# Accumulating on copied PSUM banks, an accumulating DMA for one weight sum, and a reordered opening in a hybrid decoder block

## The chip, the cores and the metric

The kernel runs on one core of a Trainium2 chip. A core has a matrix engine (TensorE, PE in the profile, with its weight loads as PEld), a vector engine (VectorE, DVE), a scalar engine (ScalarE, ACT), GpSimd (POOL) and a queue engine that issues transfers (SyncE, SP). Transfers run on 16 DMA engines, whichever queue issues them. TensorE writes its products into PSUM, eight banks of 512 float32 columns on 128 partitions. The metric is the device time of one execution in microseconds (us), as a median of runs.

## The reference

One decoder layer on 256 tokens of width 2048, in float32: a half-step SwiGLU feed-forward part, a mixer, a second half-step SwiGLU feed-forward part, and a closing norm.

```python
def swiglu_ffn(x, w_gate, w_up, w_down):
    return (jax.nn.silu(x @ w_gate) * (x @ w_up)) @ w_down
...
        x = x + FFN_RESIDUAL_SCALE * swiglu_ffn(rms_norm(x, ffn1_norm[l]), ...)
        z = rms_norm(x, mix_norm[l]) @ w_in[l]
...
        x = x + y @ w_out[l]
        x = x + FFN_RESIDUAL_SCALE * swiglu_ffn(rms_norm(x, ffn2_norm[l]), ...)
    return rms_norm(x, final_norm)
```

Between `z` and `y` stand a gated linear recurrence and a short convolution. The feed-forward width is 5632, so each of the two parts multiplies by 2048x5632, 2048x5632 and 5632x2048 matrices. These products are most of the work.

## The kernel before

**Splits.** Every float32 operand is split into a high part, rounded to the matrix engine's float32r format, and the lower part that is left. A product is three matmuls: high by high, low by high, high by low. A weight tile of 512 rows by 512 columns is a *unit*: `load` (line 155) fetches it over SP's queue, 1 MB, into a slot of the pool `raws` (three slots) or, where it is marked `kept`, of a pool of two slots (tag `kept`). `parts_of` (169) makes the high part on ACT in two casts of 128x1024 and the lower part on DVE in one subtraction of 128x2048. There are two or three slots for split tiles. `multiply` (194) runs all products with the high weight part ahead of those with the lower: 8 and 4 matmuls of 512 columns for each target.

**Products.** `product` (286) multiplies both token halves (t = 0, 1) by a column block of 512, over units. `seven` (326) does a block of 1024 columns and 1024 rows with seven products of half the size in place of eight, in the manner of Strassen and Winograd, and adds the rest of the rows with ordinary units. Its accumulators are the PSUM banks a, c, e and d. The products are numbered 0, 4, 5, 6, 2, 3, 1 in their order. Product 0 takes the weight quarter w11 into a, product 4 the sum w12 - w11 into c; then the ordinary unit b2 goes into e and c (the *two-target block* of the prediction); then product 5 adds to a, and so on. DVE makes four sums of weight quarters (128x2048 each) in a block. ACT copies a and c to SBUF four times in between (`snap`, 342: s1, s5, u2, u3), and DVE adds these at the end:

```python
        dve.tensor_tensor(u3, u3, s5, op=ALU.add)
        dve.tensor_tensor(u3, e, u3, op=ALU.add)
        dve.tensor_tensor(u2, c, u2, op=ALU.add)
        dve.tensor_tensor(s1, d, s1, op=ALU.add)
```

w11 and w12 lie in the two `kept` slots, and the slot of either goes to the next block when its last use is through.

**A feed-forward part** (`ffn`, 384) begins with one ordinary gate product of 512 columns and one ordinary up product. Ten sevens (gate and up, five times, s = 0 to 4) do the other ten column blocks, and after s = 0, 2 and 4 `down` (460) multiplies what has come about so far by the down weights: `product` for column block 0, a seven for blocks 1 and 2, `product` for block 3. That makes 13 sevens a part, 26 in all. The down products are added to the residual `xres` by DVE (`update`, 463). `settle` turns hidden tiles by PE transposes (tiles `ph`) through PSUM.

**The opening of a part.** The first products run on the unnormalised input, and their results are scaled afterwards. The sevens need the normalised input, since they add tiles of it: `norm.rows` (243) spreads the row factors over the partitions with two small products (`pb_n`) and a copy (`bc_n`); then the tiles v (line 433, both `kept` slots) are formed, scaled, split into x, and `seven_of` (308) forms the sums of the seven products' other operands (`xs`). In the program all this stands between the gate product and the up product. In the first part the gate product is `opening` (542), whose instructions are held to program order on each engine (`Engine.pinned`).

**Order.** Elsewhere the framework's planner orders each engine's instructions: it walks through time by its own estimates and gives a free engine the ready instruction that stands first in the program. The engines then run these rows in order, with semaphores. All PSUM tiles come from one pool of eight banks (79). Line 42 in the profile is the helper through which every PE, DVE and ACT instruction passes, and L164 is the load.

## Time and profile before

| | us |
|---|---|
| median of three runs (1776.07 to 1777.52) | 1777.3 |
| the profiled execution | 1779.27 |
| its span, first to last instruction | 1777.3 |
| PE busy | 1744.6 (98%) |
| DVE busy | 1494.4 (84%) |
| ACT busy | 1046.8 (59%) |
| POOL busy | 6.9 |

The span is what the profiler saw of one execution, 2.0 below that execution's time. Busy time of PE is the time in which a matmul was under way. Matmuls are pipelined, so a single one of 512 columns lasts 0.39 us in the records while in a stream one ends every 0.23. In a row of the timeline stand the start, the length, engine and line, operation, output and inputs by the program's names, shape, and the number of instructions merged; in brackets the engine's idle time ahead of it and what ended it. `ps_g_a` is bank a of a gate seven, `hi_g_p` and `lo_g_p` the split parts of a unit for one of its seven products, `hi_g_x` those of an ordinary unit; u and d stand for up and down.

### The profile page before, as it was taken

The page shows a single profiled execution, that of the slowest core. Times are in us where ns is not written, and L with a number is a line of the kernel's source. Part 1 is how long each engine was busy: PE and PEld are TensorE (multiplying, and loading weights), DVE is VectorE, ACT ScalarE, POOL GpSimd, SP SyncE. Part 2 cuts the span into 40 slices and gives each one's busy share as a digit, 9 for nine tenths or more (in the row PEclk, how much of TensorE's full clock was granted, in tenths as well). Part 3 has the DMA queues.
Part 4 walks back from the last instruction along what each step waited for, and adds up shares of the span by engine and source line. Part 5 has one row for each costly group of instructions (what it writes and reads, how often), then busy time and mean ns, then how long its engine had stood idle before and what let it go on. Part 6 is the DMA issues. An engine that isn't in the chain of part 4 may idle for free. (4 is left out here: it accounts for less than half of the span.)

```text
span 1777.3 us, 20302 instructions
## 1 busy us (share of the span) xinstructions
PE 1744.6 (98%) x8031; PEld 1441.5 (81%) x8031; DVE 1494.4 (84%) x1221; ACT 1046.8 (59%) x1342; POOL 6.9 (0%) x32
## 2 busy tenths in 40 slices
PE   7999999999999999999999999999999999999998
PEld 5787888888888888888888887887888888888886
DVE  6898989989789888688987667989899887899895
ACT  6565556656465656575765554656566664556664
POOL 1000000000000000000000000000000000000000
PEclk9999999999999999999999999999999999999999
DMA  7366655574566574456565655574566637555743
GB/s 249 132 214 212 213 189 190 190 245 155 186 196 209 172 256 166 145 188 196 175 196 170 209 189 190 190 242 157 192 214 202 209 135 259 189 190 190 257 158 106
DMA packets 173905, 343.24 MB, mean 193 GB/s; under 512 B 5621, under 2 KB 8049, under 8 KB 173681
## 3 DMA queue, kind: packets, MB, share of 16 engines
q1 hardware_dynamic: 173344, 340.82, 57.2%
q8 instruction: 63, 1.03, 0.2%
q10 hardware_dynamic: 144, 1.05, 0.2%
q14 instruction: 34, 0.27, 0.0%
q0 software_dynamic: 320, 0.07, 0.0%
HBM read 339.82 MB, written 2.10 MB: 192 GB/s over the span
## 5 line engine op out<-in xcount | busy, mean ns | idle before, releaser
L42 PE MATMUL ps_in<-xT_nm,hi_in 128*128 128x512 f32 x640 | 224.1, 395 | 0.0
L42 ACT CAST hi_g_p<-raw_g 128x1024 fp32r<-128x1024 f32 x140 | 140.5, 1048 | 123.4 <-DVE raw_g L42 40.9
L42 DVE TENSOR_TENSOR lo_g_p<-raw_g,hi_g_p 128x2048 fp32r<-128x2048 f32 x70 | 159.7, 2287 | 36.0 <-ACT hi_g_p L42 35.5
L42 ACT CAST hi_u_p<-raw_u 128x1024 fp32r<-128x1024 f32 x140 | 141.5, 1049 | 66.3 <-PE ps_u_a L42 25.9
L42 PE MATMUL ps_in<-xT_nm,lo_in 128*128 128x256 f32 x640 | 178.6, 281 | 0.6 <-DVE lo_in L42 0.6
L42 DVE TENSOR_TENSOR lo_u_p<-raw_u,hi_u_p 128x2048 fp32r<-128x2048 f32 x70 | 159.2, 2286 | 22.2 <-ACT hi_u_p L42 22.1
L42 PE MATMUL ps_d<-hi_d,h 128*128 128x512 f32 x704 | 172.2, 396 | 2.8 <-DVE h L42 2.2
L42 PEld LDWEIGHTS ps_d<-hi_d,h 128*128 128x128 f32 x704 | 132.6, 189 | 33.3 <-DVE h L42 3.0
L42 PEld LDWEIGHTS ps_in<-xT_nm,hi_in 128*128 128x128 f32 x640 | 119.8, 187 | 27.1
L42 ACT CAST hi_d<-raw_d 128x1024 fp32r<-128x1024 f32 x88 | 88.0, 1048 | 81.9 <-PE ps_u_d L42 25.3
L42 DVE TENSOR_TENSOR lo_d<-raw_d,hi_d 128x2048 fp32r<-128x2048 f32 x44 | 100.7, 2289 | 31.7 <-ACT hi_d L42 31.7
L42 PEld LDWEIGHTS ps_in<-xT_nm,lo_in 128*128 128x128 f32 x640 | 120.6, 189 | 1.4 <-DVE lo_in L42 1.1
L42 DVE TENSOR_TENSOR lo_in<-raw_in,hi_in 128x2048 fp32r<-128x2048 f32 x40 | 91.4, 2285 | 32.7 <-ACT hi_in L42 32.5
L42 ACT CAST hi_in<-raw_in 128x1024 fp32r<-128x1024 f32 x80 | 81.5, 1049 | 62.1 <-PE ps_in L42 48.8
L42 ACT CAST hi_d_p<-raw_d 128x1024 fp32r<-128x1024 f32 x84 | 84.5, 1048 | 48.2 <-DVE raw_d L42 21.0
L42 DVE TENSOR_TENSOR lo_d_p<-raw_d,hi_d_p 128x2048 fp32r<-128x2048 f32 x42 | 95.5, 2287 | 18.9 <-ACT hi_d_p L42 18.8
L42 ACT CAST hi_g_x<-raw_g 128x1024 fp32r<-128x1024 f32 x80 | 80.8, 1049 | 41.2 <-PE ps_g_c L42 19.9
L42 ACT CAST hi_u_x<-raw_u 128x1024 fp32r<-128x1024 f32 x80 | 80.6, 1049 | 37.3 <-PE ps_u_c L42 25.8
L42 DVE TENSOR_TENSOR raw_u<-raw_u,raw_u 128x2048 f32<-128x2048 f32 x40 | 91.6, 2291 | 9.4 <-DMA raw_u<-in_ffn_w_up_dram 8.7
L42 DVE TENSOR_TENSOR raw_g<-raw_g,raw_g 128x2048 f32<-128x2048 f32 x40 | 91.5, 2287 | 6.4 <-DMA raw_g<-in_ffn_w_gate_dram 5.8
L42 DVE TENSOR_TENSOR lo_g_x<-raw_g,hi_g_x 128x2048 fp32r<-128x2048 f32 x40 | 91.4, 2286 | 3.8 <-ACT hi_g_x L42 3.7
L42 DVE TENSOR_TENSOR lo_u_x<-raw_u,hi_u_x 128x2048 fp32r<-128x2048 f32 x40 | 91.5, 2287 | 3.7 <-ACT hi_u_x L42 3.1
(349 smaller groups left out, 3612.5 us busy)
## 6 DMA issues: line engine op xcount, KB each, us to landing
raw_u<-in_ffn_w_up_dram SPq DMA_DIRECT2D x88, 1024.0 KB, 5.3
raw_d<-in_ffn_w_down_dram SPq DMA_DIRECT2D x88, 1024.0 KB, 5.1
raw_g<-in_ffn_w_gate_dram SPq DMA_DIRECT2D x87, 1024.0 KB, 5.3
raw_in<-in_w_in_dram SPq DMA_DIRECT2D x40, 1024.0 KB, 5.1
raw_o<-in_w_out_dram SPq DMA_DIRECT2D x16, 1024.0 KB, 5.1
xres<-in_x_dram SPq DMA_DIRECT2D x4, 512.0 KB, 8.3
fin<-in_final_norm_dram ACTq DMA_DIRECT2D x1, 1024.0 KB, 4.7
out_dram<-xres SPq DMA_DIRECT2D x4, 256.0 KB, 2.7
```

Of the source, the lines that this page charges most:

```text
L42: ins = getattr(self.engine, name)(*args, **kwargs)
```

## The change

1. **Copied banks.** In a seven, ACT copies bank a onto bank d after product 0 and bank c onto bank e after product 4, in place of two snapshots, and the later matmuls add onto the copies. Two of the four additions on DVE go. For this the matmuls of e and d no longer begin a bank, and PSUM is divided: for each feed-forward part six `full` banks for accumulators, each written once by a dummy product of zeros, and two `part` banks for transposes and small products (`small`); for the mixer one pool of eight. In `down`, ACT writes twice the residual into the banks of an ordinary product first, and half of the result back to the residual, in place of DVE's update; the last product of the kernel keeps the old form. A down seven adds its parts to the residual one by one.
2. **The accumulating DMA.** w12 is loaded ahead of w11, and a second DMA, issued on POOL's queue, reads w11 from memory and adds it to w12. Product 4 takes this sum directly. The other three sums of a block stay on DVE.
3. **Signs.** To make that sum possible some operands are negative: the ordinary units of the second column half and one operand of the seven are split with a factor of -1, and the results of the second half are used with -1.
4. **The opening.** `norm.rows`, the tiles v and x and `seven_of` move from between the gate and the up product into the up product, one step after each of its units (`normalise`). In `opening`, units 1 to 3 are split by halves: a cast and a subtraction of half the size, twice.

```diff
--- before.py
+++ after.py
-    psum = ctx.enter_context(tc.tile_pool(name="psum", bufs=8, space=bass.MemoryType.PSUM))
-
-    def bank(name):
-        return psum.tile([P, 512], F32, tag="ps", name=name)
+    pools = {}
+
+    @contextmanager
+    def banks(name, parts):
+        with ExitStack() as st:
+            for kind, n in (("full", 8 - parts), ("part", parts)):
+                if n:
+                    pools[kind] = st.enter_context(
+                        tc.tile_pool(name=f"{kind}_{name}", bufs=n, space=bass.MemoryType.PSUM)
+                    )
+            if parts:
+                for i in range(8 - parts):
+                    pe.matmul(bank(f"first_{name}_{i}"), zeros[:, :P], zeros, start=True, stop=True)
+            else:
+                pools["part"] = pools["full"]
+            yield
+
+    def bank(name, kind="full"):
+        return pools[kind].tile([P, 512], F32, tag="ps", name=name)
+
+    def small(name):
+        return bank(name, "part")
...
+    zeros = const.tile([P, 512], F32R, name="zeros")
+    dve.memset(f32(zeros), 0.0)
...
+    ffn1_banks = ExitStack()
+    ffn1_banks.enter_context(banks("ffn1", 2))
...
         for i, e in pieces:
             if split:
                 split(i)
-            act.copy(hi[:, i:e, :], raw[:, i:e, :])
+            if minus:
+                act.activation(hi[:, i:e, :], raw[:, i:e, :], AF.Copy, scale=-1.0)
+            else:
+                act.copy(hi[:, i:e, :], raw[:, i:e, :])
             if split:
                 dve.tensor_tensor(lo[:, i:e, :], raw[:, i:e, :], f32(hi[:, i:e, :]), op=ALU.subtract)
-        if not split:
+        if minus:
+            dve.scalar_tensor_tensor(lo, raw, -1.0, f32(hi), op0=ALU.mult, op1=ALU.subtract)
+        elif not split:
             dve.tensor_tensor(lo, raw, f32(hi), op=ALU.subtract)
         return [(hi[:, j, :], lo[:, j, :]) for j in range(UK)]
...
-                pt = bank(f"pt_{self.name}_{k}")[:, :S]
+                pt = small(f"pt_{self.name}_{k}")[:, :S]
...
-    def product(w, c, us, y, name, stagger=False, between=None):
+    def product(w, c, us, y, name, stagger=False, between=None, base=None):
+
         ps = [bank(f"ps_{name}_{t}") for t in range(NT)]
+        if base:
+            for t in range(NT):
+                act.activation(ps[t], base(t), AF.Copy, scale=2.0)
...
-            begin, end = i == 0, i == len(us) - 1
+            begin, end = i == 0 and not base, i == len(us) - 1
+                multiply([(ps[t], stationary(y(u), t), begin, end) for t in range(NT)], blk, base is not None)
...
-        dve.tensor_tensor(spare, a21, a22, op=ALU.add)
+        dve.tensor_tensor(spare, a22, a21, op=ALU.subtract)
         dve.tensor_tensor(a21, a11, a21, op=ALU.subtract)
-        dve.tensor_tensor(a11, spare, a11, op=ALU.subtract)
-        dve.tensor_tensor(a12, a12, a11, op=ALU.subtract)
+        dve.tensor_tensor(a11, spare, a11, op=ALU.add)
+        dve.tensor_tensor(a12, a11, a12, op=ALU.subtract)
         for (i, q), (hi, lo) in zip(((4, spare), (5, a11), (6, a21), (2, a12)), parts):
-            act.copy(hi, q)
-            dve.tensor_tensor(lo, q, f32(hi), op=ALU.subtract)
+            if i == 5:
+                act.activation(hi, q, AF.Copy, scale=-1.0)
+                dve.scalar_tensor_tensor(lo, q, -1.0, f32(hi), op0=ALU.mult, op1=ALU.subtract)
+            else:
+                act.copy(hi, q)
+                dve.tensor_tensor(lo, q, f32(hi), op=ALU.subtract)
...
-        w11, w12 = get(r0, 0, True), get(r0, 1, True)
+        w12, w11 = get(r0, 1, True), get(r0, 0, True)
+        nc.gpsimd.dma_start(w12, at(r0, 0).rearrange("(j p) c -> p j c", p=P), accum_op=ALU.add)
...
-            blk = parts_of(raw, f"{name}_x{i}{n}")
+            blk = parts_of(raw, f"{name}_x{i}{n}", minus=n == 1)
             multiply([(ps, stationary(xs[i][1], t), b, z) for ps, t, b, z in targets], blk, True)
         product_of(0, w11, a, True)
-        s1 = snap(a, "s1")
-        dve.tensor_tensor(w11, w12, w11, op=ALU.subtract)
-        product_of(4, w11, c, True)
-        s5 = snap(c, "s5")
-        usual(0, b2, 1, (e, 1, True, not two), (c, 0, False, False))
-        dve.tensor_tensor(w11, w22, w11, op=ALU.subtract)
-        product_of(5, w11, a)
+        act.copy(d, a)
+        product_of(4, w12, c, True)
+        act.copy(e, c)
+        usual(0, b2, 1, (e, 1, False, not two), (c, 0, False, False))
+        dve.tensor_tensor(w12, w22, w12, op=ALU.add)
+        product_of(5, w12, a)
         u2 = snap(a, "u2")
         if between:
             between()
         if two:
             usual(1, b3, 1, (e, 1, False, True), (c, 0, False, False))
-        dve.tensor_tensor(w12, w22, w12, op=ALU.subtract)
-        product_of(6, w12, a)
+        dve.tensor_tensor(w11, w12, w11, op=ALU.subtract)
+        product_of(6, w11, a)
         u3 = snap(a, "u3")
         product_of(2, w22, c)
-        usual(0, a2, 0, (d, 0, True, False), (a, 1, False, False))
-        dve.tensor_tensor(w11, w21, w11, op=ALU.subtract)
-        product_of(3, w11, a, end=not two)
+        usual(0, a2, 0, (d, 0, False, False), (a, 1, False, False))
+        dve.tensor_tensor(w12, w21, w12, op=ALU.add)
+        product_of(3, w12, a, end=not two)
         if two:
             usual(1, a3, 0, (a, 1, False, True), (d, 0, False, False))
         product_of(1, w21, d)
-        dve.tensor_tensor(u3, u3, s5, op=ALU.add)
-        dve.tensor_tensor(u3, e, u3, op=ALU.add)
-        dve.tensor_tensor(u2, c, u2, op=ALU.add)
-        dve.tensor_tensor(s1, d, s1, op=ALU.add)
-        return {(1, 1): u3, (0, 1): u2, (1, 0): a, (0, 0): s1}
+        return {(1, 1): (e, u3), (0, 1): (c, u2), (1, 0): (a, None), (0, 0): (d, None)}
...
-                pt = bank(f"ph{tag}_{u}_{t}")
+                pt = small(f"ph{tag}_{u}_{t}")
...
-            norm.rows()
+            xs, sf = [], {}
+
+            def normalise(u):
+                if u == 0:
+                    norm.rows()
+                bcs = norm.bc.unsqueeze(1).to_broadcast([P, UK, S])
...
-                    sf = seven_of(
+                    sf.update(seven_of(
...
+                    ))
+
+            pu = product(wu, 0, range(4), norm.xT.__getitem__, f"u{tag}_0", between=normalise)
             xs = list(enumerate(xs))[2:]
-            pu = product(wu, 0, range(4), norm.xT.__getitem__, f"u{tag}_0")
...
-                def update(c, t, ps):
-                    xr = xres[:, t, c * CW : (c + 1) * CW]
-                    Engine.pinned = last and tag == 2 and c == NC_D - 1
-                    dve.scalar_tensor_tensor(xr, ps, 0.5, xr, op0=ALU.mult, op1=ALU.add)
-                    if last:
-                        after(c, t)
+                def columns_of(c, t):
+                    return xres[:, t, c * CW : (c + 1) * CW]
 
                 for c in (0, 3):
                     end = last and tag == 2 and c == NC_D - 1
                     ps = product(
-                        wd, c, us, hidden.get, f"d{tag}_{us[0]}_{c}", end, (lambda i: settle()) if c == 0 else None
+                        wd, c, us, hidden.get, f"d{tag}_{us[0]}_{c}", end, (lambda i: settle()) if c == 0 else None,
+                        None if end else lambda t: columns_of(c, t),
                     )
                     for t in range(NT):
-                        update(c, t, ps[t])
+                        xr = columns_of(c, t)
+                        if end:
+                            Engine.pinned = True
+                            dve.scalar_tensor_tensor(xr, ps[t], 0.5, xr, op0=ALU.mult, op1=ALU.add)
+                        else:
+                            act.activation(xr, ps[t], AF.Copy, scale=0.5)
+                        if last:
+                            after(c, t)
...
-                                update(c1, t, q[t, c1 - 1])
+                                xr = columns_of(c1, t)
+                                for part in q[t, c1 - 1]:
+                                    if part is not None:
+                                        dve.scalar_tensor_tensor(xr, part, 1.5 - c1, xr, op0=ALU.mult, op1=ALU.add)
+                                if last:
+                                    after(c1, t)
...
                 g = seven(wg, (0, 1), c0, sf, xs, f"g{tag}_{s}", keep, settle)
-                for q in ((1, 1), (0, 1), (1, 0), (0, 0)):
-                    if q == (1, 0):
-                        z = keep(f"z{tag}_{s}")
-                        act.activation(z, g[q], AF.Silu)
-                        g[q] = z
+                for q in QUADS:
+                    ps, z = g[q]
+                    if z is None:
+                        z = keep(f"z{tag}_{s}_{q[0]}")
                     else:
-                        act.activation(g[q], g[q], AF.Silu)
+                        dve.tensor_tensor(z, ps, z, op=ALU.add)
+                        ps = z
+                    act.activation(z, ps, AF.Silu, scale=-1.0 if q[1] else 1.0)
+                    g[q] = z
                 h = seven(wu, (0, 1), c0, sf, xs, f"u{tag}_{s}", keep)
-                for t, n in ((1, 1), (0, 1), (1, 0), (0, 0)):
-                    dve.tensor_tensor(g[t, n], h[t, n], g[t, n], op=ALU.mult)
+                for t, n in QUADS:
+                    ps, z = h[t, n]
+                    if z is not None:
+                        dve.tensor_tensor(z, ps, z, op=ALU.add)
+                        ps = z
+                    if n:
+                        dve.scalar_tensor_tensor(g[t, n], ps, -1.0, g[t, n], op0=ALU.mult, op1=ALU.mult)
+                    else:
+                        dve.tensor_tensor(g[t, n], ps, g[t, n], op=ALU.mult)
                     waiting.append((1 + 2 * s + n, t, g[t, n], s % 2 == 0))
...
-                blk = unit(src, f"g1_0_{u}")
+                halves_of = ((0, 2), (2, 4))
+                blk = parts_of(load(src, f"g1_0_{u}"), f"g1_0_{u}", halves_of, lambda i: None)
...
-    with tc.tile_pool(name="mixer", bufs=1) as mp, tc.tile_pool(name="mixw", bufs=2) as mw:
+    ffn1_banks.close()
+    with tc.tile_pool(name="mixer", bufs=1) as mp, tc.tile_pool(name="mixw", bufs=2) as mw, banks("mixer", 0):
...
-    ffn(2, n2, last)
+    with banks("ffn2", 2):
+        ffn(2, n2, last)
...
```

31 lines of the change are left out of this document (14 added, 17 removed).

## The prediction

> **What bounds the kernel now.** I read the head of the page first, then a table of stretches, then TensorE's (PE's) waits, and only then the timeline around the waits that matter. The first fence is the head of the page, with the span and the busy time of each engine. The second is the table of stretches: start:end, length, and for each engine its busy time and number of instructions, then granted clock, share of the DMA engines and GB/s.
>
> ```profile
> span 1777.3 us, 20302 instructions
> PE 1744.6 (98%) x8031; PEld 1441.5 (81%) x8031; DVE 1494.4 (84%) x1221; ACT 1046.8 (59%) x1342; POOL 6.9 (0%) x32
> ```
>
> ```profile
> 0.00:80.00 80.00, 63.05 (x255) 49.75 (x256) 56.45 (x71) 46.45 (x73) 5.87 (x16) 0.94 0.58 198
> 80.00:1040.00 960.00, 957.53 (x4576) 799.29 (x4575) 811.68 (x719) 571.53 (x757) 1.05 (x16) 1.00 0.58 193
> 1040.00:1130.00 90.00, 87.21 (x387) 70.61 (x386) 71.66 (x65) 50.91 (x65) 0.00 (x0) 0.98 0.54 177
> 1130.00:1750.00 620.00, 618.33 (x2739) 506.97 (x2738) 543.42 (x345) 367.18 (x426) 0.00 (x0) 1.00 0.59 200
> 1750.00:1778.00 28.00, 18.51 (x81) 14.83 (x79) 11.24 (x25) 10.77 (x23) 0.00 (x0) 0.92 0.21 76
> ```
>
> PE is busy for all but 32.7 us. In the long stretches 80 to 1040 and 1130 to 1750 it is idle for 2.5 and 1.7 us, and there VectorE (DVE) at 85 to 88% holds nobody up. So work taken from DVE inside the blocks is worth at most some 4 us. Idle time that a change could win lies in the first 80 us (17.0) and around the second feed-forward part's start (2.8); the last 28 us (some 9) are not touched. The next fence, PE's waits (who waited for whom: us in all, times, longest), names what it is made of.
>
> ```profile
> PE ps_g L42 <- DVE lo_g L42: 5.2, 3, 2.0
> PE pb_n L42 <- DVE diag_n L42: 4.5, 1, 4.5
> ...
> PE ps_u L42 <- DVE lo_u L42: 2.6, 1, 2.6
> ...
> PE ps_g_c L42 <- ACT hi_g_p L42: 1.6, 1, 1.6
> ```
>
> **The change part by part.**
>
> *Removed from DVE, placed on ScalarE (ACT).* In each of the 26 seven-product blocks one of four weight sums goes, and two of four additions on a 128x512 tile. The first three rows below are from the groups by form (busy, mean ns); the rest is the timeline of one block in the steady stretch.
>
> ```profile
> L42 DVE TENSOR_TENSOR raw_u<-raw_u,raw_u 128x2048 f32<-128x2048 f32 x40 | 91.6, 2291 | 9.4 <-DMA raw_u<-in_ffn_w_up_dram 8.7
> L42 DVE TENSOR_TENSOR u_g<-ps_g_c,u_g 128x512 f32<-128x512 f32 x10 | 6.9, 685 | 0.2 <-PE ps_g_c L42 0.2
> L42 ACT COPY s_u<-ps_u_c 128x512 f32<-128x512 f32 x10 | 5.8, 581 | 6.4 <-PE ps_u_c L42 6.4
> ```
>
> ```profile
> 242.00 0.37 SPq L164 DMA_DIRECT2D raw_u<-in_ffn_w_up_dram  x1
> ...
> 266.09 2.00 ACT L42 CAST hi_u_p<-raw_u 128x1024 fp32r<-128x1024 f32 x2 [0.69 <-DVE raw_u L42]
> ...
> 270.99 2.01 PE L42 MATMUL ps_u_c<-hi_u_p,xs 128*128 128x512 f32 x8
> ...
> 273.76 1.98 PE L42 MATMUL ps_u_e<-hi_u_x,x 128*128 128x512 f32 x8
> ```
>
> DVE is relieved of 2.29 + 2 x 0.69 = 3.7 us a block, 95 us in all. By the table it is worth nothing, because PE hides it: no matmul is saved. The products keep their number, and 12 dummy ones are added. The ACT copies are as many as the snapshots they replace, at 0.58; the base copies and the residual writes (an ACT instruction of that size for a DVE update) lie beside down products of at least three units, 24 matmuls each. If that cover were gone, each base copy would cost its 0.58. The turned signs swap an instruction for one of the same size: nothing, between a slower or faster form of some 0.1 us, hidden by the same PE cover.
>
> *The accumulating transfer.* The sum w11 + w12 is now made by a DMA from POOL's queue, which waits until the plain load of w12 has landed. Only this instruction stands on POOL's queue here. Its landing time, X, is in no row. The fence shows plain issues (queue, count, KB, median us to landing) and the queue's share of the 16 engines.
>
> ```profile
> q1 hardware_dynamic: 173344, 340.82, 57.2%
> ...
> raw_g<-in_ffn_w_gate_dram SPq DMA_DIRECT2D x87, 1024.0 KB, 5.3
> ...
> rows_first<-in_ffn_norm_dram SPq DMA_DIRECT2D x1, 8.0 KB, 1.6
> ...
> rows_many<-in_lru_out_norm_dram POOLq DMA_DIRECT2D x1, 4.0 KB, 5.7
> ```
>
> X is not under the plain 5.3. A small transfer from POOL took 5.7 against SP's 1.6, 4.1 more, part of it from the crowd of loads at the start; and an addition must also read what it adds to: at 57.2% of 1777.3 us for 340.82 MB one pass over a MB costs 3.0. So X lies between 5.3 and 5.3 + 4.1 + 2 x 3.1 = 15.6. I take 11: the load, one more pass, and two thirds of POOL's surcharge, nearer the top because loads run beside it everywhere.
>
> The Trainium skill, "DMA: Bandwidth & Descriptors", section "Anatomy of one DMA", fits about 2.0 us plus bytes at 436 GB/s, which is an estimate of 4.4 us for this 1 MiB, below the plain load's row of 5.3; by it the sum below would be about zero. The same page, "Rules for kernel authors", says that an accumulating DMA reads its destination and writes it later, which its fit does not contain and no row of this case shows.
>
> In the steady stretch X is hidden: a slot comes free for the next block's first kept load at 242.0, which lands at 247.3. Product 4 must be cast by 270.99 - 1.25, so the addition has 22 us.
>
> *The copy of c onto e.* Before, the two-target block's eight products on e (273.76) start as product 4 ends, since they begin a bank. Now they add onto a copy that starts only then: 0.58 and two hand-overs, about 1.0, with ACT and PE queued behind it. It is hidden if product 5's eight leading products stand between. Its raw sum now needs no sum before it, and its slot comes free when product 0's eight leading products are through, some 0.9 before 270.99, which leaves 3.7 us to 273.76 for a cast of 2.0; so I take 0 for 24 blocks. Uncovered it is 24 x 1.0. In the first block of each part DVE is late, and there I count 0.8.
>
> *The opening, reordered.* This is what I expect to decide. The fence is the timeline of the second part's start.
>
> ```profile
> 1082.47 0.38 PE L42 MATMUL pb_n<-diag_n,ones 128*128 128x128 f32 x2
> ...
> 1083.47 3.44 PE L42 MATMUL ps_u<-hi_u,xT_n 128*128 128x512 f32 x14
> ...
> 1083.76 0.43 DVE L42 COPY bc_n<-pb_n 128x256 f32<-128x256 f32 x1 [0.58 <-PE pb_n L42]
> ...
> 1096.39 0.68 DVE L42 TENSOR_TENSOR xs<-v,xs 128x512 fp32r<-128x512 f32 x1
> 1096.99 1.22 DVE L42 TENSOR_TENSOR x<-v,x 128x1024 fp32r<-128x1024 f32 x1
> ...
> 1102.42 1.99 ACT L42 CAST hi_g_p<-raw_g 128x1024 fp32r<-128x1024 f32 x2 [6.50 <-DMA raw_g<-in_ffn_w_gate_dram]
> ...
> 1109.45 2.01 PE L42 MATMUL ps_g_a<-hi_g_p,x 128*128 128x512 f32 x8
> ...
> 1112.21 2.02 PE L42 MATMUL ps_g_c<-hi_g_p,xs 128*128 128x512 f32 x8
> 1114.07 2.07 PE L42 MATMUL ps_g_e<-hi_g_x,x 128*128 128x512 f32 x8
> 1115.98 0.60 PE L42 MATMUL ph<-ident,sg 128*128 128x128 f32 x4
> ...
> 1118.19 2.14 PE L42 MATMUL ps_g_c<-hi_g_x,x 128*128 128x512 f32 x8 [0.24 <-ACT s_g L42]
> ```
>
> Both `kept` slots hold the v tiles until the normalisation is through. The first comes free at 1097.07, 13.3 after bc_n starts; the load lands 5.35 later, and ACT's cast begins. The second comes free 14.45 after bc_n. The change moves the pb_n products behind the 24 of the up product's first unit (24 x 0.23 = 5.5), and the six dummies stand ahead (1.4): bc_n at 1083.76 + 6.9 = 1090.7. The first slot now takes w12: free at 1104.0, loaded at 1109.4, added up at 1109.4 + X. The second takes w11, and one more 2.3 us split runs ahead of its release: 1090.7 + 16.7 = 1107.4, landed at 1112.8, half cast after 1.25, so product 0 starts at 1114.0 in place of 1109.45. Product 4 needs its cast (2.0), its lower part (2.3) and four products (0.9) after the landing, then the copy (0.8): the two-target block starts at 1115.4 + X, and not before 1114.0 + 2 x 2.76 + 0.8 = 1120.3. Before, it had done its eight e products (1.9) by 1118.19, so it stood as if started at 1116.3. Loss: X - 0.9, at least 4.0; with X = 11, 10.1.
>
> The first part's start, in the same way:
>
> ```profile
> 41.79 0.39 PE L42 MATMUL ps_g<-lo_g,xT_n 128*128 128x512 f32 x1
> 46.64 0.76 PE L42 MATMUL pb_n<-diag_n,ones 128*128 128x128 f32 x2 [4.47 <-DVE diag_n L42]
> ...
> 48.62 0.42 DVE L42 COPY bc_n<-pb_n 128x256 f32<-128x256 f32 x1 [0.89 <-PE pb_n L42]
> ...
> 72.59 2.11 PE L42 MATMUL ps_g_a<-hi_g_p,x 128*128 128x512 f32 x8
> ...
> 83.14 2.06 PE L42 MATMUL ps_g_c<-hi_g_x,x 128*128 128x512 f32 x8
> ```
>
> The gate product ends at 42.2. Splitting by halves shortens the three waits of 5.2 us in all, and the transposes, now on two banks, stall in turn; the net lies between 0 and 5.2, and I take 1.2, nearer nothing because PE is held to program order there. The 4.47 us gap closes, since the up product no longer stands behind pb_n: unit 0 from 41.0 to 46.5, bc_n at 47.8 (before 48.62). First slot at 61.1, w12 at 66.4, the two-target block at 72.4 + X; the bound by product 0 is 47.8 + 16.7 + 5.35 + 1.25 + 5.5 + 0.8 = 77.4. Before it stood at 83.14 - 1.9 = 81.2. Difference: X - 8.8, at best -3.8; with X = 11, +2.2. The six dummies here hide under the wait for x. What closes at the gap comes back as a wait for the kept slots.
>
> *Banks.* Six full and two small ones: the six and two suffice for what is alive in a block, and the pool changes at the mixer cost 0 to 2 us each where PE waits for the last banks to be read; I take 0, because the products have other banks.
>
> Sum: 10.1 + 2.2 = 12.3 on the profiled execution's 1777.3 span (1779.3 with what lies around it). The median shown, 1777.3, is 2.0 below that time, so the forecast for the median is **1790**.
>
> **The rivals.**
>
> *Faster: the row products are planned early.* If the planner finds a hole in PE's row before unit 0, bc_n comes at about 43.5 (41.0, the 2.0 from pb_n to bc_n, 0.5 for the factor) and 1083.8. Then the two-target blocks start at 68.1 + X and 1108.4 + X; with X = 6 that is 7.1 and 1.9 earlier, 1768. The 4.47 us hole speaks for it; that pb_n came behind all gate products at 1082.47, against it. It decides only while X is under about 10; at 11 it gives 1778.
>
> *No change: X is that of a plain load.* Then -3.5 and +4.4: 1778. The transfer adds up at the rate of a copy; the POOL row speaks against.
>
> *Slower: the copy onto e is uncovered.* 24 x 1.0 on top: 1814. For it: 273.76 has no other product ready in the trace. Against: product 5 is freed of a sum.
>
> *Much slower: X above 22.* Each us more counts 24 times; at 25 it is 1777 + 24 + 72, about 1875.
>
> **How the numbers follow.** Forecast 0.42 (X from 8 to 16: 1783 to 1800), early rows 0.27, no change 0.10, uncovered copy 0.14, X above 22 0.07. A measurement tells this kernel from no change at about 0.2%, 3.6 us. Faster 0.27, same 0.10, slower 0.63. The range 1766 to 1820 takes in the early rows and most of the uncovered copy, and leaves out the last case and the edges.
>
> **What would show it.** Right: PE idle for several us ahead of product 0 and product 4 in the first seven of each part, ended by an ACT cast that waits for a DMA; about 4 us idle, as now, in the steady stretches; some 95 us less DVE. Wrong: bc_n before the up product's first unit; an addition that lands in 6 us or less; gaps of 1 us in front of every e product; or first sevens that start earlier than 72.6 and 1109.5.

## The result and the profile after

The changed kernel takes 1855.65 us in the median of four runs (1854.08 to 1861.52), against 1777.41 for the kernel before beside it: a ratio of 1.0438, 95% interval 1.0401 to 1.0474. That is some 78 us slower. The forecast was 1790, the range ended at 1820, and none of the rivals stood at this time.

First the head of the page after, and PE's busy time and clock by stages. The same six stages are cut in both kernels at the same places of the program (product 0 of a part's first seven, product 0 of the gate seven after the first down products, and product 0 of the first part's third down seven). The columns are those of the prediction's table of stretches.

```profile
span 1859.7 us, 20376 instructions
PE 1775.5 (95%) x8043; PEld 1449.7 (78%) x8043; DVE 1399.6 (75%) x1125; ACT 1069.5 (58%) x1386; POOL 40.8 (2%) x58
```

The stages of the kernel before:

```profile
0.00:72.59 72.59, 57.26 (x232) 45.51 (x232) 49.04 (x61) 40.41 (x65) 5.87 (x16) 0.93 0.63 218
72.59:227.07 154.48, 151.44 (x662) 122.70 (x661) 141.94 (x117) 95.68 (x112) 0.00 (x0) 0.99 0.56 191
227.07:670.62 443.55, 443.55 (x1973) 364.88 (x1972) 386.90 (x240) 264.18 (x307) 0.00 (x0) 1.00 0.60 199
670.62:1109.45 438.83, 435.24 (x2261) 370.64 (x2260) 342.09 (x426) 253.05 (x394) 1.05 (x16) 1.00 0.56 185
1109.45:1260.83 151.38, 149.72 (x662) 121.53 (x660) 135.01 (x89) 91.07 (x106) 0.00 (x0) 1.00 0.58 195
1260.83:1777.30 516.47, 507.43 (x2249) 416.22 (x2247) 439.48 (x293) 302.44 (x362) 0.00 (x0) 1.00 0.57 192
```

The stages of the kernel after:

```profile
0.00:71.75 71.75, 57.37 (x246) 43.97 (x246) 52.82 (x89) 42.79 (x70) 7.30 (x17) 0.96 0.67 222
71.75:238.66 166.91, 155.46 (x652) 124.61 (x653) 126.19 (x80) 96.76 (x115) 3.88 (x3) 0.95 0.66 201
238.66:701.13 462.47, 452.77 (x1973) 367.77 (x1972) 355.14 (x209) 270.15 (x319) 11.65 (x9) 0.99 0.67 212
701.13:1151.11 449.98, 437.11 (x2276) 370.70 (x2274) 337.06 (x421) 257.37 (x400) 2.36 (x17) 0.99 0.55 181
1151.11:1321.59 170.48, 157.80 (x653) 125.48 (x653) 120.15 (x72) 91.39 (x109) 3.88 (x3) 0.95 0.64 197
1321.59:1859.70 538.11, 515.01 (x2248) 417.13 (x2248) 408.27 (x257) 311.01 (x378) 11.68 (x9) 0.99 0.64 201
```

DVE is relieved of 1494.4 - 1399.6 = 94.8 us, and the kernel is longer by 82.4 in these two profiled executions. The loss is everywhere but in the first stage: 12.4, 18.9, 11.2, 19.1 and 21.6 us in the other five. The third and the sixth stage, steady for the most part, where I had counted nothing, hold 18.9 and 21.6 of it. Of the 82.4, 51.5 is idle time of PE: 1859.7 - 1775.5 = 84.2, before 32.7. The rest, 30.9, is busy time of PE, though only twelve dummy products were added. The clock explains about half of that. It fell in the first sevens of either part from 0.99 and 1.00 to 0.95; over the whole span PE was busy for 47.6 us at a granted clock of 0.50, before for 16.5, and half of the difference, 15.5, is an estimate of what the slower clock added. The dummies add some 3. Where the rest comes from is not traced.

Next, what PE and ACT wait for in the kernel after (us in all, times, longest). Before, PE's largest wait was 5.2 us, and of these lines only `hi_g_p` from DMA is among ACT's larger ones, with 12.9.

```profile
PE ps_g_a L43 <- ACT hi_g_p L43: 11.6, 3, 6.0
PE ps_u_e L43 <- ACT ps_u_e L43: 10.0, 10, 1.2
PE ps_g_e L43 <- ACT ps_g_e L43: 8.8, 8, 1.7
PE ps_u_a L43 <- ACT ps_u_d L43: 7.8, 6, 2.4
PE ph L43 <- ACT u_g L43: 5.9, 2, 4.3
...
PE first_ffn L43 <- DVE xres L43: 3.0, 1, 3.0
```

```profile
ACT hi_g_p L43 <- DMA raw_g<-in_ffn_w_gate_dram: 67.3, 12, 14.5
ACT hi_u_p L43 <- DMA raw_u<-in_ffn_w_up_dram: 54.4, 11, 7.5
```

Two families stand out: PE waits for the copies onto e (18 times, 18.8 us) and onto d, and ACT waits 121.7 us for loads of the sevens' weights. The timeline of the same up seven that the prediction showed in the steady stretch has both (after, line by line in order of time):

```profile
264.91 0.37 SPq L190 DMA_DIRECT2D raw_u<-in_ffn_w_up_dram  x1
...
276.03 2.95 ACT L43 CAST hi_u_p<-raw_u 128x1024 fp32r<-128x1024 f32 x3 [6.65 <-DMA raw_u<-in_ffn_w_up_dram]
...
282.69 2.01 PE L43 MATMUL ps_u_c<-hi_u_p,xs 128*128 128x512 f32 x8
...
284.54 1.08 PE L43 MATMUL ps_u_c<-lo_u_p,xs 128*128 128x512 f32 x4
285.18 1.05 ACT L43 CAST hi_u_p<-raw_u 128x1024 fp32r<-128x1024 f32 x1 [2.37 <-DVE raw_u L43]
286.13 0.58 ACT L43 COPY ps_u_d<-ps_u_a 128x512 f32<-128x512 f32 x1
286.64 1.05 ACT L43 CAST hi_u_p<-raw_u 128x1024 fp32r<-128x1024 f32 x1
...
286.76 1.21 PE L43 MATMUL ps_u_a<-hi_u_p,xs 128*128 128x512 f32 x4 [1.14 <-ACT ps_u_d L43]
...
288.55 0.58 ACT L43 COPY ps_u_e<-ps_u_c 128x512 f32<-128x512 f32 x1
...
289.18 3.78 PE L43 MATMUL ps_u_e<-hi_u_x,x 128*128 128x512 f32 x8 [1.21 <-ACT ps_u_e L43]
...
297.67 1.10 PE L43 MATMUL ps_u_a<-hi_u_p,xs 128*128 128x512 f32 x4
```

ACT stood 6.65 us waiting for a load, and after it everything that it does in this block is late. It is the plain load of w11: issued at 264.91, when its slot came free, it landed 11.0 us later, for the transfer into w12 (259.43 to 272.97) ran beside it. The sum itself had landed by then. Before, ACT cast w11 8.9 us ahead of product 0 (259.34 against 268.23); here the lead is 3.9. Product 0 was through at 282.85 (281.77 plus 1.08), but its copy onto d runs at 286.13, behind a cast of product 5's weights for which ACT waited 2.37 us on DVE's sum; product 5 may not write bank a until then (1.14). In PE's row only four of its eight leading products stand ahead of those on e. The other four stand behind (297.67), although their cast (286.64) was through before the copy onto e began (288.55). That copy comes behind two more casts, and PE waits for it (1.21). And then the eight products on e take 3.78 where they took 1.98. The clock of these stretches:

```profile
285.18:288.59 3.41, 1.65 (x6) 0.69 (x5) 3.41 (x2) 3.41 (x5) 0.00 (x0) 1.00 0.07 8
288.59:295.42 6.83, 6.24 (x15) 4.89 (x16) 5.28 (x3) 1.53 (x3) 0.00 (x0) 0.50 0.51 160
```

The granted clock is 0.50 for 6.83 us behind the two gaps. This seven came out 5.8 us longer than before, 2.35 of it idle and the rest slow.

### The profile page after: what moved, and what is told of

Same layout as the page of the kernel before. It is cut to its first block, busy times and chain, and to the rows that moved or that the text cites. A ratio compares the mean times of both kernels' runs of the same rounds, so it can differ in the third digit from the quotient of the medians.

```text
span 1859.7 us, 20376 instructions
## 1 busy us (share of the span) xinstructions
PE 1775.5 (95%) x8043; PEld 1449.7 (78%) x8043; DVE 1399.6 (75%) x1125; ACT 1069.5 (58%) x1386; POOL 40.8 (2%) x58
## 3 DMA queue, kind: packets, MB, share of 16 engines
q8 instruction: 63, 1.03, 0.2%
## 5 line engine op out<-in xcount | busy, mean ns | idle before, releaser
L43 PE MATMUL ps_d<-hi_d,h 128*128 128x512 f32 x704 | 176.7, 400 | 3.8 <-ACT h L43 3.8
L43 PE MATMUL ps_d<-lo_d,h 128*128 128x512 f32 x352 | 88.1, 390 | 0.0
L43 PEld LDWEIGHTS ps_d<-lo_d,h 128*128 128x128 f32 x352 | 66.1, 188 | 14.4
L43 DVE TENSOR_TENSOR raw_g<-raw_g,raw_g 128x2048 f32<-128x2048 f32 x30 | 68.7, 2289 | 6.0 <-DMA raw_g<-in_ffn_w_gate_dram 5.6
L43 DVE TENSOR_TENSOR raw_u<-raw_u,raw_u 128x2048 f32<-128x2048 f32 x30 | 68.6, 2287 | 0.3
L43 PE MATMUL ps_o<-hi_o,yT 128*128 128x512 f32 x256 | 61.2, 391 | 0.0
L43 PE MATMUL ps_u_e<-hi_u_x,x 128*128 128x512 f32 x160 | 47.6, 446 | 10.0 <-ACT ps_u_e L43 10.0
## 6 DMA issues: line engine op xcount, KB each, us to landing
raw_g<-in_ffn_w_gate_dram POOLq DMA_DIRECT2D x10, 1024.0 KB, 10.3
raw_u<-in_ffn_w_up_dram POOLq DMA_DIRECT2D x10, 1024.0 KB, 12.6
```

The lines of the kernel that those rows point to most:

```text
L43: ins = getattr(self.engine, name)(*args, **kwargs)
```

## The experiments

The runs in one table (ratio to the kernel before on the same chip, with its interval; the last column is the ratio's excess on 1777.4). "C" are the copied banks d and e, "A" the accumulating transfer, "O" the reordered opening, "B" the two pools of banks with their dummies and the copied base and ACT-written results of the down products. All runs made from the changed kernel also keep the turned signs, w12 loaded ahead of w11 and the other closing additions of the sevens.

| run | what it holds | ratio | 95% interval | us |
|---|---|---|---|---|
| the change | C A O B | 1.0438 | 1.0401 to 1.0474 | +77.9 |
| e1_sum_on_dve | C O B | 1.0179 | 1.0162 to 1.0196 | +31.8 |
| e2_snapshots | A O B | 1.0356 | 1.0337 to 1.0375 | +63.3 |
| e3_neither | O B | 1.0111 | 1.0086 to 1.0137 | +19.7 |
| e4_copy_d_only | copy onto d, A O B | 1.0362 | 1.0346 to 1.0377 | +64.3 |
| e5_opening_alone | O | 0.9993 | 0.9980 to 1.0007 | -1.2 |
| e6_banks_alone | B | 1.0064 | 1.0041 to 1.0088 | +11.4 |
| e7_plain_second | A as a plain write, O B | 1.0143 | 1.0122 to 1.0165 | +25.4 |
| e8_half_accum | half of A, O B | 1.0176 | 1.0153 to 1.0200 | +31.3 |
| e9_first_opening_only | O in the first part | 0.9959 | 0.9942 to 0.9975 | -7.3 |
| e10_four_pieces | A in four, O B | 1.0382 | 1.0359 to 1.0406 | +67.9 |
| e11_no_base | O, two pools and dummies | 1.0101 | 1.0078 to 1.0124 | +18.0 |
| e12_first_order_only | O in the first part, no halves | 0.9977 | 0.9966 to 0.9988 | -4.1 |
| e13_late_light | A late but light, O B | 1.0287 | 1.0261 to 1.0313 | +51.0 |
| e14_heavy_unread | A heavy but not waited for, O B | 1.0377 | 1.0359 to 1.0395 | +67.0 |
| e15_no_dummies | O, two pools | 1.0107 | 1.0092 to 1.0122 | +19.0 |

### Taking the change apart: copies and the accumulating transfer

My theory from the trace after was that both causes act: gaps at the copies, and loads made late by the accumulating transfer. The first four runs take away one or the other. First, the sum made by DVE:

```diff
-        nc.gpsimd.dma_start(w12, at(r0, 0).rearrange("(j p) c -> p j c", p=P), accum_op=ALU.add)
...
         act.copy(d, a)
+        dve.tensor_tensor(w12, w12, w11, op=ALU.add)
         product_of(4, w12, c, True)
```

> The changed kernel, with the sum w11 + w12 made on DVE after two plain loads, in place of the accumulating transfer; the copies onto d and e stay. My theory, read from the trace after: two causes. Each copy onto e leaves PE a gap of 0.8 to 1.2 us, and the accumulating transfer makes the loads beside it late (8 to 13 us for 5.3), so that ACT is behind and a second gap opens ahead of product 5, after which the granted clock falls to 0.5 or 0.6 for some 6 us. By it this run keeps the single gaps in some 20 blocks and loses the double ones: 1800 to 1815, clock 0.99. Rival 1, the accumulating transfer alone is to blame and with loads in time the copies are covered: 1775 to 1785. Rival 2, the copies alone are to blame: 1845 to 1860.

Measured: 1811.48, clock 0.99, as expected. Second, both copies undone:

```diff
-        act.copy(d, a)
+        s1 = snap(a, "s1")
...
-        act.copy(e, c)
-        usual(0, b2, 1, (e, 1, False, not two), (c, 0, False, False))
+        s5 = snap(c, "s5")
+        usual(0, b2, 1, (e, 1, True, not two), (c, 0, False, False))
...
-        usual(0, a2, 0, (d, 0, False, False), (a, 1, False, False))
+        usual(0, a2, 0, (d, 0, True, False), (a, 1, False, False))
...
+        dve.tensor_tensor(u3, u3, s5, op=ALU.add)
-        return {(1, 1): (e, u3), (0, 1): (c, u2), (1, 0): (a, None), (0, 0): (d, None)}
+        return {(1, 1): (e, u3), (0, 1): (c, u2), (1, 0): (a, None), (0, 0): (d, s1)}
```

> The changed kernel with the accumulating transfer kept and both copied banks undone: s1 and s5 are copied to SBUF as before, e and d begin with a start, and DVE adds s1 and s5 at the end. My theory of two causes: the gaps ahead of the e products go, and with them the low clock; what stays are late loads at the two openings (some 10 us) and the first down products, 1785 to 1805. Rival 1, the transfer alone is to blame: 1845 to 1860. Rival 2, the copies alone are to blame: 1775 to 1785.

Measured: 1841.11. This is a miss: I had thought that the transfer costs little once no copy stands in PE's way. Third, both edits together:

> The changed kernel with neither: the sum w11 + w12 on DVE after plain loads, and SBUF copies of a and c as before. What is left of the change is the reordered opening, the copied and ACT-written banks of the down products, the banks in two pools and the turned signs. My theory: these are worth little, 1772 to 1785. Rival 3, the opening or the two small banks cost much by themselves (the idle time of some 8 us around the first down products and the pool changes at the mixer): 1790 to 1810.

Measured: 1799.18, so the third rival was right and 20 us lie in neither. Fourth, of the edits of e2_snapshots only the one for e:

> The changed kernel with the copy onto e alone undone (s5 goes to SBUF and DVE adds it); the copy onto d and the accumulating transfer stay. It splits the copies: the copy onto d has four products between it and its use. My theory: as the run with both copies undone, within 4 us, 1785 to 1805, for the copy onto e makes the gaps. If instead the wait of product 5 on bank a (for ACT to have read it for d) is the costly one, this run stays above 1825.

Measured: 1843.36, 2.3 above e2_snapshots, so as expected the copy onto e is the costly one of the two; my number for both was too low by the transfer's share.

What follows: from e3_neither to e2_snapshots the accumulating transfer costs 43.6 us, and the copies on top of it 14.6 more (12.1 without it, from e3_neither to e1_sum_on_dve). Between the profiled executions of e3_neither and e2_snapshots, 26.2 of 41.8 us lie in the third and the sixth stage and 15.8 in the second and the fifth, which hold the first sevens. In e1_sum_on_dve the waits for the copy onto e are shorter, 0.34 each in the up sevens, since ACT has its loads in time.

```profile
PE ps_u_e L43 <- ACT ps_u_e L43: 3.4, 10, 0.4
```

Where the transfer hurts without any copied bank is seen in the waits of e2_snapshots, PE's first and ACT's behind them:

```profile
PE ps_u_c L43 <- ACT s_u L43: 10.8, 7, 2.9
PE ps_g_c L43 <- ACT s_g L43: 8.2, 6, 2.8
...
ACT hi_g_p L43 <- DMA raw_g<-in_ffn_w_gate_dram: 70.1, 12, 13.7
```

The products on e now start at once, but the ordinary unit's products on c may not write c until ACT has copied it to SBUF, and that copy stands behind casts that were late. The wait has moved from one target of the block to the other.

### The 20 us that stay: the opening and the banks

The opening alone, on the kernel before (the second part of the edit is the split by halves, as in the change):

```diff
-            norm.rows()
...
-            for u in range(4):
+            def normalise(u):
+                if u == 0:
+                    norm.rows()
...
+            pu = product(wu, 0, range(4), norm.xT.__getitem__, f"u{tag}_0", between=normalise)
```

> The kernel before with the reordered opening alone: row products and normalisation inside the up product, and the first gate product's units split by halves. It takes apart the 20 us that stay when neither the copies nor the accumulating transfer are there (run e3_neither). Theory: in the second part the row products come one unit later still than I had counted, and product 0 of the first seven waits some 5 us more for its kept slots, with a low clock behind it, while the first part gains about 1: 1782 to 1790. Rival, the banks are all of the 20: 1775 to 1779. Rival, the opening is all of it: 1795 to 1800.

Measured: 1777.01, no difference. And the rest alone, e3_neither with the opening turned back by the same lines:

> The kernel of run e3_neither with the old opening: what is left of the change is the two pools of banks with their dummy products, the base copied into the banks of the down products, their results written by ACT, and the turned signs. Theory: the pool changes at the mixer (3.0 and 1.0 us) and the waits of the transposes for one of two small banks around the first down products (some 8 us) cost PE 12 us together, in part doubled by the clock: 1786 to 1796. Rival, the opening is all of the 20: 1776 to 1781.

Measured: 1788.90. So the two cost nothing and 11.4 apart and 19.7 together: the banks also take away what the opening gains in the first part. The trace shows that gain and its loss. First the transposes, the row products and product 0 in the run with the opening alone, one pool of eight banks (before: `pb_n` at 46.64, product 0 at 72.59):

```profile
25.78 1.03 PE L42 MATMUL pt_n<-ident,xres 128*128 128x128 f32 x8
...
41.39 0.38 PE L42 MATMUL pb_n<-diag_n,ones 128*128 128x128 f32 x2
...
63.55 3.78 PE L42 MATMUL ps_g_a<-hi_g_p,x 128*128 128x512 f32 x8 [4.70 <-ACT hi_g_p L42]
...
1101.81 3.78 PE L42 MATMUL ps_g_a<-hi_g_p,x 128*128 128x512 f32 x8 [5.98 <-ACT hi_g_p L42]
```

Then the same in the run with two pools and no dummies (e15_no_dummies, below):

```profile
28.96 0.60 PE L43 MATMUL pt_n<-ident,xres 128*128 128x128 f32 x4
...
30.43 0.83 PE L43 MATMUL pt_n<-ident,xres 128*128 128x128 f32 x4 [0.87 <-DVE xT_n L43]
...
46.24 0.46 PE L43 MATMUL pb_n<-diag_n,ones 128*128 128x128 f32 x2 [0.31 <-DVE diag_n L43]
...
71.51 3.78 PE L43 MATMUL ps_g_a<-hi_g_p,x 128*128 128x512 f32 x8 [5.13 <-ACT hi_g_p L43]
```

With one pool eight transposes go through in 1.03. With two small banks the second four wait until the first four's banks are read, with PE held to program order, and eight take 30.43 + 0.83 - 28.96 = 2.30. Product 0 comes at 71.51 in place of 63.55. In the second part product 0 stands behind a gap of some 6 us in both, and there the opening loses. The two runs that take the banks apart further are e3_neither without the copied base, and that without the dummies too:

```diff
-                        None if end else lambda t: columns_of(c, t),
...
-                            act.activation(xr, ps[t], AF.Copy, scale=0.5)
+                        dve.scalar_tensor_tensor(xr, ps[t], 0.5, xr, op0=ALU.mult, op1=ALU.add)
```

> The run e3_neither (1799) with the down products as before: a bank is begun with a start, DVE adds the result to the residual, and no copied base. The two pools of banks, the dummy products and the reordered opening stay. Theory: the pools are what takes away the opening's gain and adds the waits at the pool changes and for the small banks, and the base costs 0 to 5: 1793 to 1800. Rival, the base and the writes on ACT, in order with the casts, cost most of the 20: 1777 to 1786.

Measured: 1796.90. The difference of 1.7 lies within the intervals, so no cost of the base is shown. Then the lines of the dummies removed from `banks`:

```diff
-            if parts:
-                for i in range(8 - parts):
-                    pe.matmul(bank(f"first_{name}_{i}"), zeros[:, :P], zeros, start=True, stop=True)
-            else:
+            if not parts:
```

> The run e11_no_base (1797: two pools, reordered opening, no copied base) without the twelve dummy products. Theory: PE stands 3.0 us at the dummies of the second part and 1.6 at those of the first, and the reordered opening is late by as much; without them the rest of the two pools (the pool changes, and two banks for transposes) stays: 1787 to 1793. Rival, the dummies are all of it: 1776 to 1780. Rival, they cost nothing, since the products behind them wait as long for the same tiles: 1795 to 1800.

Measured: 1797.52. The last rival was right. Without the dummies the gate product waits as long as they did, 3.26 us for 3.0. The row below names ACT, but DVE's last reading of the mixer's banks also ended just then, at 1063.94; I read both waits as one for the banks of the pool before.

```profile
1064.09 3.88 PE L43 MATMUL ps_g<-hi_g,xT_n 128*128 128x512 f32 x16 [3.26 <-ACT junk_n L43]
```

Around the first down products the hidden tiles' transposes go through the same two banks. Before, sixteen of them stood in a row at 1199.05 to 1200.96 without a wait; in e6_banks_alone PE stands between them:

```profile
1202.76 1.04 PE L43 MATMUL ph<-ident,u_g 128*128 128x128 f32 x8
1207.41 0.66 PE L43 MATMUL ph<-ident,z 128*128 128x128 f32 x4 [3.61 <-ACT u_g L43]
```

Where the loss lies is seen by stages: against e5_opening_alone, e15_no_dummies is longer by 8.0, -0.2, 1.0, 7.9, 2.6 and 0.8 us. That is the first opening, the stage with the mixer and the second opening, and the one with the second part's first down products. No run takes away the turned signs, the order of the two loads or the sevens' closing additions; but these also work in the third and the sixth stage, where hardly anything is lost, so I put the loss down to the pools.

### What the accumulating transfer does

Two runs change its kind and size, both on e2_snapshots. In one, the transfer writes w11 over w12:

```diff
-        nc.gpsimd.dma_start(w12, at(r0, 0).rearrange("(j p) c -> p j c", p=P), accum_op=ALU.add)
+        nc.gpsimd.dma_start(w12, at(r0, 0).rearrange("(j p) c -> p j c", p=P))
```

> The run e2_snapshots (1841: accumulating transfer kept, copies undone) with that transfer made a plain one: w11 is written over w12 in the same place of POOL's queue, behind the same load. It leaves the sum w11 + w12 out, so the output isn't the reference's. Theory: it is the adding that is long (13 us of landing, with the loads beside it at 11), a plain one lands in 6 to 8 us, and the time falls to 1800 to 1812. Rival: any second transfer into the slot, behind the first and on POOL's queue, makes the block's loads late: 1830 to 1845.

Measured: 1804.11. In the other it adds half of the rows and DVE the other half:

```diff
-        nc.gpsimd.dma_start(w12, at(r0, 0).rearrange("(j p) c -> p j c", p=P), accum_op=ALU.add)
+        nc.gpsimd.dma_start(w12[:, :2], at(r0, 0)[: 2 * P].rearrange("(j p) c -> p j c", p=P), accum_op=ALU.add)
...
+        dve.tensor_tensor(w12[:, 2:], w12[:, 2:], w11[:, 2:], op=ALU.add)
         product_of(4, w12, c, True)
```

> The run e2_snapshots with half of the sum made by the accumulating transfer (the first 256 of the 512 rows, 512 KB) and the other half by DVE. Theory: landing time and the delay of the loads beside go with the bytes, so some 7 us for 13, and the lead that is lost falls by more than half, since up to some 5 us of delay a block's casts have room: 1803 to 1820. Rival, the cost is a fixed one of each accumulating transfer: 1835 to 1845.

Measured: 1808.26. Both as the theory had it. The profile pages show a difference that goes with it; the queue that POOL feeds (packets, MB, share of 16 engines) and its issues (count, KB, median us to landing), first after, then e7_plain_second:

```profile
q0 software_dynamic: 14048, 27.34, 8.4%
...
raw_g<-in_ffn_w_gate_dram POOLq DMA_DIRECT2D x10, 1024.0 KB, 10.3
raw_u<-in_ffn_w_up_dram POOLq DMA_DIRECT2D x10, 1024.0 KB, 12.6
```

```profile
q0 software_dynamic: 7392, 27.34, 4.2%
...
raw_u<-in_ffn_w_up_dram POOLq DMA_DIRECT2D x10, 1024.0 KB, 6.7
```

The accumulating MB goes in about twice as many packets and takes twice the engines' time: 8.4% of 1859.7 us over 26 transfers is 6.0 us each, against 4.2% of 1804.8, 2.9 us. The plain loads issued while one was under way took 9.6 us in the median of e2_snapshots (67 of them), the others 5.2; in e7_plain_second 7.7 and 5.25. Cutting the transfer into four was to tell whether the loads only stand behind one long transfer:

```diff
-        nc.gpsimd.dma_start(w12, at(r0, 0).rearrange("(j p) c -> p j c", p=P), accum_op=ALU.add)
+        for j in range(UK):
+            nc.gpsimd.dma_start(w12[:, j], at(r0, 0)[j * P : (j + 1) * P], accum_op=ALU.add)
```

> The run e2_snapshots (1841) with its accumulating transfer cut into four of 256 KB each. In run e2_snapshots the accumulating queue holds the 16 DMA engines for 8.4% of the span, in run e7_plain_second, with as many MB, for 4.2%. Theory: the engines' time per MB makes everything late, the loads beside included, and pieces have the same bytes: 1832 to 1850. Rival, the plain loads only stand behind one long transfer in a queue, and get through between the pieces: 1805 to 1825.

Measured: 1846.84, nothing won, as the theory had it: the loads issued beside the pieces took 9.5 us in the median (74 of them).

That left open whether it costs that the sum is late, or that the loads beside it are. One run makes the first without the second:

```diff
-        nc.gpsimd.dma_start(w12, at(r0, 0).rearrange("(j p) c -> p j c", p=P), accum_op=ALU.add)
+        for _ in range(4):
+            nc.gpsimd.dma_start(w12[:, 0, :8], at(r0, 0)[:P, :8])
```

> The run e2_snapshots (1841) with the accumulating transfer replaced by four small plain ones (4 KB each) to the same slot, one after the other on POOL's queue. The sum w11 + w12 is left out, so the output isn't the reference's. The slot is ready late, by four small landings (I expect 8 to 12 us in all), but the 16 engines are not loaded. Theory: what costs is that the plain loads beside an accumulating transfer are late, not that the sum is: 1798 to 1810. Rival, the sum's own lateness costs: 1825 to 1845.

Measured: 1827.98. The other, on e3_neither, makes the second without the first:

```diff
+    unread = nc.dram_tensor("unread", (UK * P, CW), F32, kind="Internal").ap()
...
+        nc.gpsimd.dma_start(unread[:P, :8], w12[:, 0, :8])
+        nc.gpsimd.dma_start(unread, at(r0, 0), accum_op=ALU.add)
```

> The run e3_neither (1799: the sum on DVE) with an accumulating transfer of the same w11 beside it, into a tensor in memory that nobody reads, started at the same place of POOL's queue, behind the load of w12. Nobody waits for it, but it loads the 16 engines. Theory: the loads beside it are late all the same, and the time is near that of e2_snapshots: 1822 to 1845. Rival, the sum's own lateness costs and the load on the engines doesn't: 1798 to 1808.

Measured: 1843.65. My theory of a single cause falls: each alone costs most of the 43.6, 31.3 and 47.3. They don't add up; I take it that both use up the same lead. The plain loads issued beside took 5.4 us in the median of e13_late_light and 9.4 in e14_heavy_unread, so only the second makes them late.

Three reservations: in e13_late_light the slot was ready 14.7 us late in the median (9.1 to 19.1), more than the 12.0 of the accumulating transfer; e14_heavy_unread has one wait that no other run has, 6.44 us at transposes ahead of a late down product with a low clock around it, which makes it some 8 us too long; and there DVE's sum waited in four blocks, 12.6 us in all, for the 4 KB read that starts the transfer.

The pattern over the stages is nearer the loads beside. Against e3_neither, the third and the sixth stage together lose 26.2 us in e2_snapshots, 15.1 in e13_late_light (9.6 of them in two blocks) and 34.5 in e14_heavy_unread, some 26 without the one wait. The second and the fifth, with the first sevens, lose 15.8, 17.0 and 4.3. So in the steady stretches it is chiefly the loads beside, and at the starts the late sum; the shares are not settled further.

### A version that beats both

The opening's gain in the first part and its loss in the second are separate places, so the reordered opening was put into the first part alone. Against e5_opening_alone:

```diff
+            if not opening:
+                norm.rows()
...
-                if u == 0:
+                if u == 0 and opening:
                     norm.rows()
...
-            pu = product(wu, 0, range(4), norm.xT.__getitem__, f"u{tag}_0", between=normalise)
+            if not opening:
+                for u in range(4):
+                    normalise(u)
+            pu = product(wu, 0, range(4), norm.xT.__getitem__, f"u{tag}_0", between=normalise if opening else None)
```

> The kernel before with the reordered opening in the first part alone; the second part keeps the old order. In the trace of run e5_opening_alone the first part's product 0 starts at 63.55 (before 72.59) and the first part comes out 7.9 us ahead; the second part's product 0 stands behind a gap of 5.98 us and gives 3.7 back. Theory: the two are separate, so this run keeps the 7.9: 1768 to 1773 where before is 1778. Rival, what the first part gains is given back by waits further on: 1775 to 1779.

Measured: 1771.65, ratio 0.9959 (0.9942 to 0.9975): faster than both kernels. Its product 0 in the first part:

```profile
41.73 0.38 PE L42 MATMUL pb_n<-diag_n,ones 128*128 128x128 f32 x2
...
63.88 3.78 PE L42 MATMUL ps_g_a<-hi_g_p,x 128*128 128x512 f32 x8 [4.69 <-ACT hi_g_p L42]
```

And without the split by halves:

```diff
-                halves_of = ((0, 2), (2, 4))
-                blk = parts_of(load(src, f"g1_0_{u}"), f"g1_0_{u}", halves_of, lambda i: None)
+                blk = unit(src, f"g1_0_{u}")
```

> The run e9_first_opening_only without the split by halves: in the first part alone, only the row products and the normalisation stand inside the up product. It tells which half of the opening gains. Theory: the wait of 4.47 us ahead of the row products closes and the normalisation begins earlier, so most of the gain is the order's: 1771 to 1775. Rival, the split by halves is all of it: 1776 to 1779, or slower.

Measured: 1774.19, ratio 0.9977 (0.9966 to 0.9988). The order gives 4.1 of the 7.3 us; the 3.2 that are left for the halves lie within the two intervals and are not shown.

## Why the prediction was wrong

*DVE's relief* was right in size (94.8 for 95). Its worth was not measured apart: only the first stage came out shorter, by 0.8 us.

*X, the landing time*, was right in number: 11 forecast, 10.3 to 12.6 measured by kind of weight. In part that is luck. In e7_plain_second the three plain transfers on POOL's queue that no load was issued beside took 5.7 to 6.7, so POOL's surcharge is nearer 1 than the 2.7 taken; loads beside make up the difference. The fit of the Trainium skill, "DMA: Bandwidth & Descriptors", section "Anatomy of one DMA", gives an estimate of 4.4 for it; the three accumulating transfers of e2_snapshots that no load was issued beside took 8.8 to 9.1, so the measurement decides against that fit for this kind of transfer.

*"In the steady stretch X is hidden"* is the step that failed most. The transfer cost 43.6 us in all, some 26 of them in the steady stretches; in the stages of the first sevens the sum had counted with X. The step held the sum against PE's need of product 4, 22 us away, and in the steady stretches PE does get product 4 in time. But ACT runs its casts and copies in a fixed order, its lead is made by casting these very tiles early, and the step left out that the plain loads beside the transfer become late too (9.6 us for 5.2), w11's among them, which ACT needs first. When ACT has waited 6.65 us at the head of a block, PE's later products wait for ACT's copies.

*"The copy of c onto e ... I take 0 for 24 blocks"* failed as well. Eight products of product 5 were to stand in between; PE's fixed row has four there, and the other four behind the products on e, though their weights were cast in time. The copy onto e also stands behind casts in ACT's row. That the 18 waits come to 18.8 us, near the price of 1.0 that I gave for an uncovered one, is luck: with the loads in time (e1_sum_on_dve) the four cover most of it, and 0.34 is left in the up sevens. This is the rival of the uncovered copy, half covered; its 24 was too much for the copies alone (12 to 15), and its 1814 lacked the rest.

*"Banks ... I take 0"* failed: 11.4 alone, and with the reordered opening 18 to 20. I had asked whether two banks are enough for what is alive, and not how fast a row of transposes goes through two of them (2.30 for 1.03); and the wait at the second part's pool change, 3.0 to 3.3, is above the 0 to 2 that I named.

*The opening* came out near the sum. The two-target block of the first part starts at 83.50 (forecast 72.4 + 11 = 83.4). In the second part it starts 1162.89 - 1096.84 = 66.05 us after the gate product, before 1116.3 - 1059.7 = 56.6: 9.4 later, where the sum had 10.1 less 1.4 for the dummies. Two errors cancel there for the most part: bc_n started later than worked out, 1.6 in the first part (49.36 for 47.8) and 2.2 in the second, and the transfer took 8.6 us in both openings, not 11. What I didn't see is that one pool would have given the first part 8 us: the rival with the row products planned early had that mechanism, and e9_first_opening_only shows it. A second omission is the clock: behind the gaps ahead of product 0 (5.32 and 5.98 us) the first sevens run at a granted clock of 0.50 for some 4 us.

So the sum of 12.3 held its named term, the openings, and put at nothing three terms that measure some 26 (of the transfer's 43.6), 14.6 and 11 to 20. One sum in the rivals is wrong as well: by the prediction's own formulas an X of 25 costs 24.1 and 16.2 in the two openings, so that rival stands at 1889 and not 1875.

## What to carry to other kernels

A transfer or a copy is not hidden because the engine at the end has time until its need: look for the engine in between that runs in a fixed order (ACT here), and ask what lead it lives on and what stands behind the late instruction in its row. Count what a new transfer does to the loads beside it, not only its own landing. And where a shared pool of banks is divided, time the longest burst that must go through the smaller part.

## What was not expected of the hardware

An accumulating DMA of 1 MB took 6.0 us of the 16 engines' time and about twice the packets, against 2.9 for a plain one on the same queue. It landed in some 9 us where no load was issued during it (three of the 26 in e2_snapshots) and in 9.4 to 14.3 otherwise; the plain loads issued during it took 9.6 in place of 5.2.

The granted clock dropped to 0.50 for 6.83 us after two gaps of 1.14 and 1.21 us with 1.21 of work between. It did the same behind a single gap of 1.87, which ended at 551.34:

```profile
547.99:551.41 3.42, 1.55 (x8) 0.95 (x6) 3.42 (x2) 1.65 (x3) 0.00 (x0) 1.00 0.00 0
551.41:558.24 6.83, 6.45 (x15) 4.57 (x16) 6.83 (x4) 3.28 (x4) 0.00 (x0) 0.50 0.46 154
```

A single gap of 0.80 in the next up seven left it at 1.00, and so did one of 3.05 ahead of the second part's dummies, at 1095.34. In the trace after, the clock drops at multiples of 3.41 us from one another, and in the 3.41 us ahead of each of its ten drops before the end PE was busy for 0.60 to 1.81. The gap of 3.05 lies across two such stretches, with 1.57 and 2.21 busy, so the busy time alone doesn't settle it. The Trainium skill, "TensorE: Matmul & The Clock Gate", Part 1, has the clock halved after at least one idle window of some 3.4 us. Here PE was partly busy in each of these stretches, and single gaps as short as 1.87 were enough; for gaps this short the measurement decides.
